# The second rope product of the attention scores: 64 rows or all 128

## The chip, the cores and the metric

The kernel runs on one core of one Trainium2 chip. The metric is the time of one execution on the device in microseconds; several runs are made and their median counts.

## The reference, cut to what matters

The reference is one layer of a decoder: two token mixers side by side (multi-head latent attention and a gated delta rule), merged by gates, then a SwiGLU feed-forward layer, each behind a normalised and modulated input. There is one sequence of 512 tokens, the model width is 2048, and all inputs are f32. The change touches one sum, the attention scores:

```python
MLA_HEADS = 8; QK_NOPE = 128; QK_ROPE = 64; Q_BLOCK = 128
for i in range(T // Q_BLOCK):
    q0, k_end = i * Q_BLOCK, (i + 1) * Q_BLOCK
    s = (jnp.einsum('bqhd,bkhd->bhqk', q_nope[:, q0:k_end], k_nope[:, :k_end])
         + jnp.einsum('bqhr,bkr->bhqk', q_pe[:, q0:k_end], k_pe[:, :k_end]))
    s = s.astype(jnp.float32) * scale
    ...
    p = jax.nn.softmax(jnp.where(mask, s, -jnp.inf), axis=-1).astype(v.dtype)
    outs.append(jnp.einsum('bhqk,bkhd->bqhd', p, v[:, :k_end]))
```

Each head has 128 "nope" features of its own and 64 "rope" features whose key side, `k_pe`, is shared by all heads. The second einsum, over the 64 rope features, is where the change lies.

## The kernel before, in words

All products run on TensorE in the type `float32r`. To keep f32 accuracy a value is split into a high part that `float32r` holds exactly and a low part, the remainder (`hilo`, L235, `halves`, L257). A product of two split operands is then three matmuls: high by high, high by low, low by high (`three`, L273).

The rope features are laid out differently. The 64 features of one head fill only half of the 128 partitions, so the kernel uses the other half for the low part of the queries. For an even head, `qpT[h]` (the tile named `qe`, L1086 to L1092) holds the high part in rows 0 to 63 and the low part, brought there by a DMA, in rows 64 to 127. For an odd head (`qo`) it is the other way round. The keys' side, the tile `kp`, has `kpT[0]`, the high part of `k_pe` in both halves, and `kpT[1]`, its low part in both halves (L1033 to L1042). So one matmul over 128 rows with `kpT[0]` gives the high and the low part of the queries times the high part of the keys. A second matmul gives the high part of the queries times the low part of the keys: before the change it takes only the 64 rows `r` that hold the high part.

Attention is a generator, `attention` (L1142). It runs over 32 items (8 heads by 4 blocks of 128 queries), and one step of it issues the value product of item i-3 (`values`, tile `yT`), the transposes of item i-2 (`transposes`, tile `pT`), the softmax of item i-1 (`softmax`, tiles `sm` and `P`) and the scores of item i (`scores`, tile `sc`). The scores are five matmuls into one PSUM tile: three over the nope features (`qn` by `kn`) and two over the rope features (`qe` or `qo` by `kp`). The moving operand has 256, 256, 384 or 512 columns for the four query blocks of a head.

The generator does not run by itself. Weights stream through units of matmuls (`Unit`, `Driver`, L35 to L127), and after every `GROUP` = 12 matmuls of units the driver advances each open generator by one step:

```python
            for m in u.mms:
                m()
                self.count += u.weight
                if self.count >= GROUP:
                    self.count -= GROUP
                    self.pump()
```

During attention these units are first those of the query and key products (`qk_unit`, tile `qk`), then those of the second gate's logits (tile `gb`), whose four PSUM banks are emptied by ScalarE (`gate_done`, tile `sg`, L1223). Between them stand a few one-column products (`adac`). TensorE, GpSimd and the queue on SyncE keep the order in which the program issues; VectorE and ScalarE are ordered by the tile scheduler. Behind attention come the output products `ya`, `yb` and `wo`, and then the feed-forward layer, most of it as products named `m`. Before it, the gated delta rule uses products on 32x32 and 64x64 parts of the array (tiles `M` and `X`) for its triangular inverse.

Every matmul is recorded at L155, the line of the helper that keeps the order, so the groups of the profile are told apart by their tiles.

Of the kernel before, what the change touches and what calls it, by code (L numbers as in the profile page):

```python
# [171 lines left out]
def block_kernel(ctx: ExitStack, tc: tile.TileContext, a: dict, out, out_t):  # L172
# [17 lines left out]
    def S(s, dt=F32):  # L190
        return slots.tile([P, 512], dt, tag="s", name=nm(s))

    def PS(s):
        return psum.tile([P, 512], F32, tag="ps", name=nm(s))
# [10 lines left out]
    mm = nc.tensor.matmul  # L205

    def tok(j):
        return slice(j * P, (j + 1) * P)
# [26 lines left out]
    def hilo(src, name, scale=None):  # L235
        hi, lo = S(name + "h", F32R), S(name + "l", F32R)
        n = src.shape[1]
        if scale is None:
            nc.scalar.copy(hi[:, 0:n], src)  # L239
            nc.vector.tensor_tensor(lo[:, 0:n], src, hi[:, 0:n].bitcast(F32), ALU.subtract)  # L240
        else:
            nc.scalar.activation(hi[:], src, AF.Copy, scale=scale)
            nc.vector.scalar_tensor_tensor(lo[:], src, scale, hi[:].bitcast(F32), op0=ALU.mult, op1=ALU.subtract)
        return hi, lo
# [750 lines left out]
    kpT = []  # L995
# [49 lines left out]
    qpT = {}  # L1045
# [96 lines left out]
    def attention():  # L1142
        items = [(h, qb) for h in range(8) for qb in range(4)]
        n = len(items)
        box = [dict() for _ in items]
        yps = {}

        def scores(i):
            h, qb = items[i]
            N = max(qb + 1, 2) * P  # L1150
            ps = PS("sc")
            for q, k in ((0, 0), (0, 1), (1, 0)):
                mm(ps[:, 0:N], QN[h][q][:, tok(qb)], KN[h][k][:, 0:N], start=q == k, stop=False)
            r = slice(64, 128) if h % 2 else slice(0, 64)
            mm(ps[:, 0:N], qpT[h][:, tok(qb)], kpT[0][:, 0:N], start=False, stop=False)
            mm(ps[:, 0:N], qpT[h][r, tok(qb)], kpT[1][r, 0:N], start=False, stop=True)
            box[i]["ps"] = ps
            if qb == 3:
                del QN[h], KN[h]

        def softmax(i):
            h, qb = items[i]
            N = (qb + 1) * P
            ps = box[i].pop("ps")
            m, s, r = (sm[:, i, j:j + 1] for j in range(3))
            nc.vector.tensor_tensor(ps[:, tok(qb)], ps[:, tok(qb)], neg, ALU.add)
            nc.vector.tensor_reduce(m, ps[:, 0:N], AX.X, ALU.max)
            nc.vector.tensor_scalar(m, m, -scale, None, op0=ALU.mult)
            p = S("P")
            nc.scalar.activation(p[:, 0:N], ps[:, 0:N], AF.Exp, bias=m, scale=scale, accum_out=s)  # L1170
            nc.vector.reciprocal(r, s)
            nc.vector.tensor_scalar(p[:, 0:N], p[:, 0:N], r, None, op0=ALU.mult)
            box[i]["p"] = p

        def transposes(i):
            h, qb = items[i]
            N = (qb + 1) * P
            p = box[i].pop("p")
            ps = PS("pT")
            for kb in range(qb + 1):  # L1180
                nc.tensor.transpose(ps[:, tok(kb)], p[:, tok(kb)], ident)
            s = S("pT")
            (nc.scalar.copy if i % 2 else nc.vector.tensor_copy)(s[:, 0:N], ps[:, 0:N])
            box[i]["pT"] = s

        def values(i):
            h, qb = items[i]
            s = box[i].pop("pT")
            if qb == 0:
                yps[h] = PS("yT")  # L1190
            for kb in range(qb + 1):
                mm(yps[h][:, tok(qb)], V[h // 4][kb][:, tok(h % 4)], s[:, tok(kb)], start=kb == 0, stop=kb == qb)
            if qb == 3:
                yT[h] = hilo(yps.pop(h)[:], "y")
                if h % 4 == 3:
                    del V[h // 4]

        for i in range(n + 3):
            if i < n:
                while items[i][0] not in QN or items[i][0] not in qpT:  # L1200
                    yield
                if i == 0:
                    yield 2
            if i >= 3:
                values(i - 3)
            if 2 <= i < n + 2:
                transposes(i - 2)
            if 1 <= i < n + 1:
                softmax(i - 1)
            if i < n:  # L1210
                scores(i)
            yield
# [1188 lines left out]
```

## Time and profile before

| | us |
|---|---|
| median of 3 runs | 2759.52 |
| lowest and highest run | 2758.9 and 2764.0 |
| the profiled execution's own time | 2765.03 |
| its span, first to last instruction | 2763.3 |

| engine | busy us | share |
|---|---|---|
| PE (TensorE matmuls) | 2733.2 | 99% |
| PEld (weight loads, beside them) | 2344.3 | 85% |
| DVE (VectorE) | 2016.5 | 73% |
| ACT (ScalarE) | 1171.4 | 42% |
| POOL (GpSimd) | 254.6 | 9% |

How to read it: times are microseconds from the first instruction unless marked ns. A row of the order of time gives start, duration, engine, line, operation, tiles (out<-in), the part of the array that is used (rows*columns), the output's shape and a count; neighbours of one kind are merged. What stands in brackets is the idle time of the engine before the row and who ended it. Matmuls are pipelined: the durations of neighbours overlap and their ends are modelled, so the distance between starts tells what one costs. A group of instructions has busy time, the mean ns of one, and the idle time before it. A tile's view has minimum, median and maximum of the duration in ns. A row of waits has the total, how many, and the longest. A row of windows has the stretch, its length, then the busy time of PE, PEld, DVE, ACT and POOL (with counts), the granted TensorE clock, the DMA share and GB/s.

### The profile page before, as it was taken

To read this page: it belongs to the slowest core of one execution; us is meant where nothing else is said; L and a number is where in the kernel's file an instruction comes from. 1 tells how busy PE (TensorE), PEld (TensorE's weight loads), DVE (VectorE), ACT (ScalarE), POOL (GpSimd) and SP (SyncE) were. 2 spreads that over 40 slices of the span, in tenths; PEclk is the share of its full clock that TensorE was granted. 3 is DMA by queue.
4 is the path that set the end of the run, shared out by engine and by line. 5 is a ranking of instruction groups with operands and counts; after the bars stand their busy time and mean duration, and the time that the engine had idled before them with its cause. 6 is when DMAs were issued, how large, how long until landed. Compare 5 with 4: busy or idle time off the path is not lost.

```text
span 2763.3 us, 39805 instructions
## 1 busy us (share of the span) xinstructions
PE 2733.2 (99%) x14860; PEld 2344.3 (85%) x14860; DVE 2016.5 (73%) x3192; ACT 1171.4 (42%) x1652; POOL 254.6 (9%) x340
## 2 busy tenths in 40 slices
PE   9999999999999999999999999999999999999998
PEld 7888788888888888888999888888888888998997
DVE  8884657676967546784487877778777867878866
ACT  3443432542344333222374444444444445446545
POOL 0000011102000000001000000000000103113113
PEclk9999999999999999999999999999999999999999
DMA  9896556646755648885464655665665668569565
GB/s 358 305 362 200 153 162 180 188 147 181 210 156 161 202 131 289 298 300 200 158 187 135 199 199 198 206 216 198 203 208 191 214 207 193 114 197 204 128 188 166
DMA packets 308924, 558.98 MB, mean 202 GB/s; under 512 B 40085, under 2 KB 109877, under 8 KB 308601
## 3 DMA queue, kind: packets, MB, share of 16 engines
q1 hardware_dynamic: 259848, 461.09, 51.6%
q0 software_dynamic: 29088, 67.42, 9.4%
q10 hardware_dynamic: 19792, 27.92, 2.9%
q8 instruction: 116, 1.90, 0.3%
q14 instruction: 80, 0.65, 0.1%
HBM read 474.52 MB, written 80.76 MB: 201 GB/s over the span
## 4 chain that ended last, share of the span: by engine, by line
PE 93%; DVE 2%; DMA 2%; issue 1%; ACT 1%; POOL 0%; SPq 0%; ACTq 0%; DVEq 0%; POOLq 0%
PE m L155 38%; PE wo L155 6%; PE gb L155 6%; PE v L155 4%; PE gu L155 3%; PE z L155 3%; PE ya L155 3%; PE k L155 3%; PE dn L155 3%; PE q L155 3%; PE yb L155 3%; PE s L155 3%; PE qk L155 2%; PE ckv L155 2%; PE cq L155 2%; PE ga L155 1%
## 5 line engine op out<-in xcount | busy, mean ns | idle before, releaser
L263 ACT CAST hi<-raw 128x1024 fp32r<-128x1024 f32 (+1 forms) x274 | 285.1, 1042 | 663.9 <-DMA raw<-in_w_in_dram 143.7
L264 DVE TENSOR_TENSOR lo<-raw,hi 128x1024 fp32r<-128x1024 f32 (+1 forms) x274 | 337.1, 1232 | 305.9 <-ACT hi L263 289.5
L1727 ACT CAST hi<-raws 128x512 fp32r<-128x512 f32 (+1 forms) x240 | 218.4, 910 | 328.3 <-PE m L155 264.5
L1728 DVE TENSOR_TENSOR lo<-raws,hi 128x512 fp32r<-128x512 f32 (+1 forms) x240 | 247.8, 1045 | 85.2 <-ACT hi L1727 84.7
L155 PE MATMUL m<-xh,hi 128*128 128x256 f32 x896 | 256.4, 286 | 4.2 <-ACT xh L239 2.3
L155 PE MATMUL m<-xl,hi 128*128 128x256 f32 x896 | 256.6, 286 | 3.9 <-DVE xl L240 3.9
L155 PE MATMUL m<-xh,lo 128*128 128x256 f32 x896 | 256.3, 286 | 0.9 <-DVE lo L1903 0.9
L435 DVE CUSTOM_DVE_ANT_0 rawm<-rawm,cbc 128x1024 f32<-128x1024 f32 x192 | 233.0, 1233 | 8.1 <-DMA rawm<-in_w_mod_dram 7.5
L155 PE MATMUL m<-hi,h2h 128*128 128x512 f32 x480 | 190.4, 397 | 0.0
L155 PE MATMUL m<-hi,h2l 128*128 128x512 f32 x480 | 187.2, 390 | 0.0
L155 PE MATMUL m<-lo,h2h 128*128 128x512 f32 x480 | 186.8, 389 | 0.0
L155 PEld LDWEIGHTS m<-xl,hi 128*128 128x128 f32 x896 | 174.8, 195 | 4.8 <-DVE xl L240 4.8
L155 PEld LDWEIGHTS m<-xh,hi 128*128 128x128 f32 x896 | 174.5, 195 | 4.9 <-ACT xh L239 2.7
L155 PEld LDWEIGHTS m<-xh,lo 128*128 128x128 f32 x896 | 174.6, 195 | 1.3 <-DVE lo L1903 1.3
L1727 ACT CAST hi<-sums 128x1024 fp32r<-128x1024 f32 x80 | 84.2, 1053 | 108.8 <-PE m L155 103.9
L1728 DVE TENSOR_TENSOR lo<-sums,hi 128x1024 fp32r<-128x1024 f32 x80 | 97.8, 1223 | 24.1 <-ACT hi L1727 23.6
L155 PE MATMUL wo<-mh,hi 128*128 128x512 f32 (+1 forms) x320 | 111.2, 347 | 0.0
L155 PE MATMUL wo<-ml,hi 128*128 128x512 f32 (+1 forms) x320 | 110.9, 347 | 0.0
L155 PE MATMUL wo<-mh,lo 128*128 128x512 f32 (+1 forms) x320 | 110.9, 347 | 0.0
L1902 ACT CAST hi<-sums 128x1024 fp32r<-128x1024 f32 x64 | 67.1, 1048 | 96.8 <-PE m L155 77.3
L155 PEld LDWEIGHTS m<-hi,h2l 128*128 128x128 f32 x480 | 90.0, 188 | 19.3
L155 PEld LDWEIGHTS m<-lo,h2h 128*128 128x128 f32 x480 | 90.3, 188 | 17.7
(537 smaller groups left out, 7307.8 us busy)
## 6 DMA issues: line engine op xcount, KB each, us to landing
raws<-in_w_gate_up_dram SPq DMA_DIRECT2D x400, 256.0 KB, 3.5
rawm<-in_w_mod_dram SPq DMA_DIRECT2D x192, 512.0 KB, 5.4
raw<-in_w_in_dram SPq DMA_DIRECT2D x144, 512.0 KB, 4.6
raws<-in_w_down_dram SPq DMA_DIRECT2D x128, 256.0 KB, 4.0
raw<-in_w_o_dram SPq DMA_DIRECT2D x40, 512.0 KB, 4.6
s_dram<-raws POOLq DMA_DIRECT2D x80, 256.0 KB, 2.3
raws<-s_dram SPq DMA_DIRECT2D x80, 256.0 KB, 3.2
rawa<-in_w_in_dram SPq DMA_DIRECT2D x32, 512.0 KB, 4.2
```

The source lines that it names most:

```text
L155: return self.tc.keep_in_program_order(f(*args, **kwargs))
L263: nc.scalar.copy(hi[:], raw[:])
L264: (lo_eng or nc.vector).tensor_tensor(lo[:], raw[:], hi[:].bitcast(F32), ALU.subtract)
L435: r = nc.vector.tensor_tensor_reduce(raw, raw, c, 1.0, 0.0, ALU.mult, ALU.add, parts[:, k, half:half + 1])
L1727: nc.scalar.copy(hi[:], src)
L1728: nc.vector.tensor_tensor(lo[:], src, hi[:].bitcast(F32), ALU.subtract)
L1902: nc.scalar.copy(hi[:], src)
```

## The change

In `scores`, the second rope matmul takes all 128 rows of `qpT[h]` and `kpT[1]`, as the first one does with `kpT[0]`. It thereby adds the product of the queries' low part with the keys' low part, a term that was left out before. Nothing else differs.

```diff
-            r = slice(64, 128) if h % 2 else slice(0, 64)
-            mm(ps[:, 0:N], qpT[h][:, tok(qb)], kpT[0][:, 0:N], start=False, stop=False)
-            mm(ps[:, 0:N], qpT[h][r, tok(qb)], kpT[1][r, 0:N], start=False, stop=True)
+            for k in range(2):
+                mm(ps[:, 0:N], qpT[h][:, tok(qb)], kpT[k][:, 0:N], start=False, stop=k == 1)
```

## The prediction

> **What bounds the kernel now.** I read the page first: busy shares, the slices, the chain that ended last.
>
> ```profile
> span 2763.3 us, 39805 instructions
> PE 2733.2 (99%) x14860; PEld 2344.3 (85%) x14860; DVE 2016.5 (73%) x3192; ACT 1171.4 (42%) x1652; POOL 254.6 (9%) x340
> PE 93%; DVE 2%; DMA 2%; issue 1%; ACT 1%; POOL 0%; SPq 0%; ACTq 0%; DVEq 0%; POOLq 0%
> ```
>
> TensorE is busy 99% of the span and makes 93% of the chain. A nanosecond taken from its stream counts unless another engine is late there. So the question is local: what do the 32 score products cost on TensorE, and is anything close behind?
>
> Next the tile view of the scores (sc) gives their shapes and their place, the windows of that stretch who is busy beside them, and the waits of TensorE over the whole span what it ever stops for.
>
> ```profile
> L155 PE MATMUL sc<-knl,qnh x32: 279/310/387, 853.9 to 1006.9; 128*128 128x256 f32 x16, 128*128 128x384 f32 x8, 128*128 128x512 f32 x8
> L155 PE MATMUL sc<-kp,qe x32: 278/380/500, 854.1 to 985.2; 128*128 128x256 f32 x8, 64*128 64x256 f32 x8, 128*128 128x384 f32 x4, 64*128 64x384 f32 x4
> L155 PE MATMUL sc<-kp,qo x32: 278/381/498, 873.0 to 1007.7; 128*128 128x256 f32 x8, 64*128 64x256 f32 x8, 128*128 128x384 f32 x4, 64*128 64x384 f32 x4
> ...
> 853.00:873.00 20.00, 20.00 (x108) 16.36 (x107) 16.26 (x49) 11.56 (x27) 2.08 (x4) 1.00 0.59 174
> 893.00:910.00 17.00, 17.00 (x86) 13.55 (x86) 14.34 (x38) 7.65 (x17) 0.00 (x0) 1.00 0.88 290
> 853.70:1008.20 154.50, 154.16 (x795) 124.36 (x793) 92.42 (x259) 59.71 (x130) 1.82 (x4) 1.00 0.50 162
> ...
> PE m L155 <- DVE xl L240: 3.9, 4, 1.2
> PE gb L155 <- ACT sg L1223: 0.3, 1, 0.3
> ```
>
> There are 32 score products of five matmuls each, 16 with 256 columns, 8 with 384, 8 with 512. The fifth is the one that works on 64 rows (64*128). In their 154.5 us TensorE is busy 154.16 at full clock (1.00), VectorE 92.42, ScalarE 59.71. The only wait of TensorE recorded there is the 0.3 us on sg.
>
> **What the change adds and removes.** Instructions: none either way. Each engine has the same list in the same order in both programs; the only rows that differ are the fifth score matmuls and their weight loads, which become 128*128. No wait, buffer or transfer moves: the added half of qe or qo is what the fourth matmul, just before, reads already, and the added half of kp was written long before.
>
> What a 64-row matmul costs must be read from the distance between starts, since the durations of pipelined matmuls overlap. The order of time around one score product of each width:
>
> ```profile
> 931.21 0.28 PE L155 MATMUL sc<-knh,qnl 128*128 128x256 f32 x1
> 931.33 0.59 PE L155 MATMUL sc<-kp,qe 128*128 128x256 f32 x2
> 931.85 0.50 PE L155 MATMUL gb<-hh,hi 128*128 128x512 f32 x1
> 932.19 0.39 PE L155 MATMUL gb<-hl,hi 128*128 128x512 f32 x1
> 932.42 0.40 PE L155 MATMUL gb<-hh,lo 128*128 128x512 f32 x1
> ...
> 941.79 0.34 PE L155 MATMUL sc<-knh,qnl 128*128 128x384 f32 x1
> 941.97 0.71 PE L155 MATMUL sc<-kp,qe 128*128 128x384 f32 x2
> 942.61 0.50 PE L155 MATMUL gb<-hh,hi 128*128 128x512 f32 x1
> 942.94 0.40 PE L155 MATMUL gb<-hl,hi 128*128 128x512 f32 x1
> ...
> 907.19 0.39 PE L155 MATMUL sc<-knh,qnl 128*128 128x512 f32 x1
> 907.42 0.83 PE L155 MATMUL sc<-kp,qe 128*128 128x512 f32 x2
> 908.18 0.50 PE L155 MATMUL gb<-hh,hi 128*128 128x512 f32 x1
> 908.52 0.40 PE L155 MATMUL gb<-hl,hi 128*128 128x512 f32 x1
> ```
>
> The row "x2" holds the fourth (128 rows) and the fifth matmul (64 rows) together. At 256 columns a full-row step is 931.33 - 931.21 = 0.12, more exactly half of 0.23, since 512 columns take 932.42 - 932.19 = 0.23. The pair takes 931.85 - 931.33 = 0.52 where two full-row steps would take 0.23: 0.29 too much. At 384 columns: 942.61 - 941.97 = 0.64 against 2 x 0.175 (a step is 0.18 by the rows, 0.75 x 0.23 by the columns): 0.29. At 512: 908.18 - 907.42 = 0.76 against 0.46: 0.30. The excess does not grow with the columns, so it is a fixed cost of going in and out of 64 rows, not a slower stream.
>
> Then the first matmul behind it also takes too long: 932.19 - 931.85 = 0.34, 942.94 - 942.61 = 0.33 and 908.52 - 908.18 = 0.34 for 512 columns that cost 0.23. That is another 0.10. Does this second part belong to the 64 rows, or to any change of product? Two other places tell:
>
> ```profile
> 540.93 0.39 PE L155 MATMUL v<-hh,lo 128*128 128x512 f32 x1
> 541.25 2.08 PE L155 MATMUL M<-T,LT 64*64 64x64 f32 x32
> 543.25 0.50 PE L155 MATMUL v<-hh,hi 128*128 128x512 f32 x1
> 543.59 0.39 PE L155 MATMUL v<-hl,hi 128*128 128x512 f32 x1
> ...
> 1040.81 0.39 PE L155 MATMUL gb<-hh,lo 128*128 128x512 f32 x1
> 1041.04 0.39 PE L155 MATMUL ya<-yh,hi 128*128 128x512 f32 x1
> 1041.26 0.39 PE L155 MATMUL ya<-yl,hi 128*128 128x512 f32 x1
> ```
>
> Going from gb to ya, both on 128 rows, costs nothing: 0.23, then 0.22. Going from v into the 64*64 products costs 541.25 - 540.93 = 0.32 in place of 0.23, and the first matmul after them takes 543.59 - 543.25 = 0.34. So both tolls, about 0.09 on entering and 0.11 after leaving, come with the change of the array's shape; the rest, about 0.20, lies on the 64-row matmul itself. With 128 rows all of it should go.
>
> Sum: 16 x (0.29 + 0.11) + 8 x (0.29 + 0.10) + 8 x (0.30 + 0.10) = 6.4 + 3.1 + 3.2 = 12.7 us. Twice the next work is not a 512-column product but adac:
>
> ```profile
> 936.68 1.05 PE L155 MATMUL adac<-ones,acc 128*128 128x1 f32 x8
> ```
>
> There I drop the 0.10, since no row shows it behind that kind: 12.5 us. Bounds of the leaving toll: if it stays in all 30 other items, 9.5; nothing lets it be more than the row shows.
>
> Off this comes what TensorE cannot keep. Two places have cover only just long enough:
>
> ```profile
> 986.87 0.39 PE L155 MATMUL gb<-hh,lo 128*128 128x512 f32 x1
> 987.60 0.50 PE L155 MATMUL gb<-hh,hi 128*128 128x512 f32 x1 [0.34 <-ACT sg L1223]
> ...
> 905.97 0.35 DVE L1172 TENSOR_SCALAR P<-P,sm 128x256 f32<-128x256 f32 x1
> 906.52 0.38 PE L155 MATMUL pT<-kc,P 128*128 128x128 f32 x2
> ```
>
> At 987.60 TensorE waits for ScalarE to empty a bank of the gate product. It already stands still there, so the 0.4 us won in the last score before it only lengthens that wait: minus 0.4. At 906.52 the transposes of P start 906.52 - 906.32 = 0.20 us after VectorE finished P. VectorE is at 16.26 of 20 and 14.34 of 17 us there, 81 and 84%, and it runs in step with TensorE (it begins a softmax when a score is done), so most of its work comes earlier too. Price between 0 (it follows fully) and 4.7 us (all 12 items up to 908 us lose their 0.39). I take 0.4, one item's gain: the cover is thin only at such single rows, and VectorE would still be at about 92% (14.34 over 17 less 3.6 items of 0.4). Behind the stretch nothing consumes the lead: buffers free earlier and loads start earlier by the same amount, and no further TensorE wait of weight exists but those of the m products at the end (3.9 us in all), which follow TensorE's own order.
>
> Net: 12.5 - 0.4 - 0.4 = 11.7 us. The profiled execution took 2765.03 us (span 2763.3 and 1.7 around it), 5.5 over the median of the runs, 2759.52; it would take 2753.3. The part of the program that the change touches is the same in each run, so the median goes to 2759.5 - 11.7 = **2747.8 us**.
>
> **Rivals.**
>
> *VectorE paces the first twelve items.* If the softmax and the splits for the qk units cannot follow, those keep their old pace: 12.5 - 4.7 - 0.4 = 7.4 us, time 2752.1. For it: the 0.20 us of cover, and 81 to 84% busy. Against it: no wait of TensorE on VectorE is recorded there now, and VectorE's own idle time ends mostly when TensorE gives it something.
>
> *Nothing happens.* One matmul with fewer rows costs what a full one costs, and the excess comes from something that stays, such as the reading of kp. Then the time stays at 2759.5. The groups by shape speak against it:
>
> ```profile
> L155 PE MATMUL sc<-kp,qe 64*128 64x256 f32 x8 | 3.0, 380 | 0.0
> L155 PE MATMUL sc<-kp,qe 128*128 128x256 f32 x8 | 2.2, 279 | 0.0
> ```
>
> Both read kp and qe over 256 columns; the 64-row one is 101 ns longer. The Trainium skill, "TensorE: Matmul & The Clock Gate", section "Why this matters for your kernels", has the rule behind this rival: a single matmul with small K takes the same time as one with K=128. By it the sum would be zero; the trace does not bear it out between full-row neighbours.
>
> *Slower: new waits halve the clock.* At its end the kernel shows what short waits can do. There TensorE waits on the m products (the rows above, up to 1.2 us each), and in the window around it the clock falls:
>
> ```profile
> 2338.20:2348.40 10.20, 8.14 (x43) 7.93 (x44) 7.99 (x13) 4.70 (x8) 0.00 (x0) 0.67 0.27 75
> ```
>
> A mean of 0.67 over 10.2 us loses 3.4 us. If TensorE now overruns P in the first twelve items and stands for a microsecond at several of them, each such place could cost 3.4 us. The gain is used up at four of them; slower by more than 5.5 us needs 11.7 + 5.5 = 17.2 us, five or more: 2765 us. Against it: a wait can only grow to what TensorE has won since VectorE was last level, 0.4 us an item, and 0.4 us waits such as that at 987.60 left the clock at 1.00.
>
> **How the numbers follow.** A measurement of this kernel can tell 0.2%, 5.5 us, from no change. The forecast (10 to 13 us won) gets 0.76, VectorE's pace 0.14, nothing 0.07, slower 0.03. The first two are faster by over 0.2% (7.4 us is 0.27%): 0.90; same 0.07; slower 0.03. The range: its low end takes the full 12.5 (2747.0) and 3 us for one half-clock stretch less at the kernel's end; the runs before lie 5.1 us apart (2758.9 to 2764.0), so this is within their play. Its high end takes in the VectorE rival (2752.1) and about 2 us of that play: 2744 to 2754.
>
> **What would show each step.** Right: all 64 kp rows 128*128; the pair at 256 columns takes 0.23 instead of 0.52 and the next first step 0.23 instead of 0.34; the stretch from first to last score shrinks from 154.5 to about 143 us; the sg wait grows from 0.3 to about 0.7. VectorE's pace shows as waits of pT on P in the qk half with the gb half fully shortened. The forecast is wrong if the pair shortens but the 0.34 stays, if new TensorE waits in the stretch sum to over 4 us, or if the stretch shrinks and time behind 1008 us grows.

## The result and the profile after

| | kernel before, us | changed kernel, us |
|---|---|---|
| median of 7 runs each | 2764.42 | 2755.55 |
| lowest and highest run | 2758.9 and 2766.03 | 2751.16 and 2756.55 |
| span of the profiled execution | 2763.3 | 2751.1 |

The ratio of the runs is 0.9968, with a 95% interval from 0.9957 to 0.998: the change makes the kernel faster by about 9 us, between 5.5 and 12. The direction was forecast, and 11.7 us lies within that interval. The time was not: 2755.55 lies over the range of 2744 to 2754. The median of before, 2759.52 from three runs when the prediction was made, is 2764.42 with the four later ones.

The page of the changed kernel, its first lines:

```profile
span 2751.1 us, 39805 instructions
PE 2719.3 (99%) x14860; PEld 2341.4 (85%) x14860; DVE 2016.4 (73%) x3192; ACT 1170.4 (43%) x1652; POOL 255.0 (9%) x340
```

The number of instructions is the same, VectorE and ScalarE are busy as before, and TensorE is busy 13.9 us less (2733.2 before). The tile view of the scores shows the new shape, and the order of time around three score products (the same as were shown of before) the new steps:

```profile
L155 PE MATMUL sc<-kp,qe x32: 278/308/398, 853.9 to 976.2; 128*128 128x256 f32 x16, 128*128 128x384 f32 x8, 128*128 128x512 f32 x8
...
926.57 0.40 PE L155 MATMUL sc<-kp,qe 128*128 128x256 f32 x2
926.80 0.40 PE L155 MATMUL gb<-hh,hi 128*128 128x512 f32 x1
927.04 0.40 PE L155 MATMUL gb<-hl,hi 128*128 128x512 f32 x1
...
936.75 0.51 PE L155 MATMUL sc<-kp,qe 128*128 128x384 f32 x2
937.10 0.39 PE L155 MATMUL gb<-hh,hi 128*128 128x512 f32 x1
937.33 0.40 PE L155 MATMUL gb<-hl,hi 128*128 128x512 f32 x1
...
904.41 0.62 PE L155 MATMUL sc<-kp,qe 128*128 128x512 f32 x2
904.88 0.40 PE L155 MATMUL gb<-hh,hi 128*128 128x512 f32 x1
905.11 0.39 PE L155 MATMUL gb<-hl,hi 128*128 128x512 f32 x1
```

The pair of rope products takes 0.23, 0.35 and 0.47 us, where it took 0.52, 0.64 and 0.76, and the first matmul behind it 0.24, 0.23 and 0.23 instead of 0.33 to 0.34. That is 0.39 or 0.40 us an item at every width, as added up.

The waits of TensorE in this stretch show what was not kept:

```profile
PE gb L155 <- ACT sg L1222: 0.7, 1, 0.7
PE pT L155 <- DVE sm L1167: 0.7, 1, 0.7
PE pT L155 <- DVE P L1171: 0.6, 2, 0.4
```

The wait on sg grew from 0.3 to 0.7, and the transposes of P now wait on VectorE, 1.3 us in all. The sum of the stretch stands between two rows, the first score and the first `ya` (before: 853.70 and 1041.04; from the unrounded starts the distance is 187.33):

```profile
853.45 0.36 PE L155 MATMUL sc<-knh,qnh 128*128 128x256 f32 x1
...
1030.52 0.39 PE L155 MATMUL ya<-yh,hi 128*128 128x512 f32 x1
```

1030.52 - 853.45 = 177.07: the stretch is 10.26 us shorter. From the first score to the last the distance is 144.08 us instead of 154.01.

### The profile page after: what moved, and what is told of

It is laid out like the page before. It is cut to its first block, busy times and chain, and to the rows that moved or that the text cites. A ratio compares the mean times of both kernels' runs of the same rounds, so it can differ in the third digit from the quotient of the medians.

```text
span 2751.1 us, 39805 instructions
## 1 busy us (share of the span) xinstructions
PE 2719.3 (99%) x14860; PEld 2341.4 (85%) x14860; DVE 2016.4 (73%) x3192; ACT 1170.4 (43%) x1652; POOL 255.0 (9%) x340
## 4 chain that ended last, share of the span: by engine, by line
PE 92%; DVE 3%; DMA 2%; issue 1%; ACT 1%; POOL 0%; SPq 0%; DVEq 0%; ACTq 0%; POOLq 0%
PE m L155 38%; PE wo L155 6%; PE gb L155 6%; PE v L155 4%; PE gu L155 3%; PE z L155 3%; PE ya L155 3%; PE k L155 3%; PE dn L155 3%; PE q L155 3%; PE yb L155 3%; PE s L155 3%; PE ga L155 2%; PE ckv L155 2%; PE cq L155 2%
## 5 line engine op out<-in xcount | busy, mean ns | idle before, releaser
L155 PEld LDWEIGHTS m<-hi,h2h 128*128 128x128 f32 x480 | 90.1, 188 | 18.4 <-DVE euvw L1744 0.8
```

The costliest lines, as they stand in the source:

```text
L155: return self.tc.keep_in_program_order(f(*args, **kwargs))
```

## The experiments

Two measures are used. The **stretch** is the distance from the first score to the first `ya` in the trace of one execution; it came out as 187.33 us in all three traces of the unchanged kernel that were taken, so beside it differences of a few tenths can be read. The changed kernel waits more in it, and its three traces lie 0.63 us apart: smaller differences from it, of one trace each, are not read. The **time** of whole runs spreads over 7 us and more, so only ratios of several runs count there.

| kernel | stretch, us | against 187.33 |
|---|---|---|
| before, three traces | 187.33 | 0 |
| changed, three traces | 177.07, 176.49, 176.44 | -10.26 to -10.89 |
| 96 rows | 176.49 | -10.84 |
| 32 rows | 187.08 | -0.25 |
| 64-row matmul twice | 192.17 | +4.84 |
| 128-row matmul twice | 180.32 | -7.01 |
| 64-row matmul first | 187.06 | -0.27 |
| 128 rows from head 3 on | 180.14 | -7.19 |
| changed, one item more of distance | 176.26 | -11.07 |
| changed, P scaled on ScalarE | 176.79 | -10.54 |

**Both kernels again, on two chips.** No edit.

> The kernel before, unchanged, to see how its runs lie. Theory clock: the runs differ by how long TensorE stood at half clock, so a span grows by 0.0005 x 2763 = 1.4 us for each 0.001 by which the mean clock is lower if half of the work is lost in it, up to 2.8 us if all of it is; runs at 0.997 near 2759, runs at 0.994 or 0.995 near 2766, and the median of many runs near 2764, not 2759.5. Rival draw: the clock is the same in short and long runs, the spread is of another source, and the median of many goes back to 2759.5.

> The changed kernel, unchanged. Theory toll: 10 us less than the kernel before in the same rounds, ratio 0.9963 with an interval from 0.995 to 0.998; runs from 2750 to 2757. Rival nothing: ratio within 0.2% of 1.

The kernel before had a median of 2765.45 us (11 runs, 2763.11 to 2771.26) beside 2764.68 (21 runs, from 2759.77) of the same program in the same rounds. The changed kernel had 2753.79 (5 runs, 2749.19 to 2757.74), ratio 0.9963, interval 0.995 to 0.9975. Then the same on another chip:

> The kernel before once more, on whichever chip comes. If the low runs of 2758.9 and 2759.5 were the luck of three draws, the median is again 2764 to 2766 and at most one run in ten lies below 2760. If they belong to the chip or the day, another median can come out, down to 2759.5.

> The changed kernel once more beside it: 10 to 11 us under the kernel before of the same rounds, ratio 0.996, whatever its level.

Before: 2764.1 (10 runs, 2761.27 to 2769.97) beside 2763.91 (15 runs, from 2761.72). Changed: 2753.6 (6 runs, 2750.19 to 2757.22), ratio 0.9968, interval 0.9955 to 0.998. Of these 57 runs of the kernel before, on two chips, one lies under 2760 us. The two low runs among the three that the prediction started from, 2758.9 and 2759.52, were a rare draw, or came from a chip that was not met again; that can't be told apart. The mean clock of the 57 runs goes with their time as the theory said (2769.2 us on average at 0.994, 2766.3 at 0.995, 2763.0 at 0.997), but the runs at 0.997 lie near 2763, not 2759 as it had said.

Where the spread of the runs arises can be seen in two traces of the same program. Windows of the feed-forward layer, first of `base` and then of `base_b`:

```profile
1490.80:2330.00 839.20, 839.20 (x3838) 697.35 (x3837) 651.46 (x762) 383.79 (x466) 87.06 (x140) 1.00 0.63 203
2330.00:2763.00 433.00, 409.60 (x3088) 395.19 (x3086) 334.62 (x530) 214.84 (x325) 78.27 (x94) 0.97 0.62 164
```

```profile
1490.80:2330.00 839.20, 839.12 (x3832) 696.23 (x3831) 650.53 (x761) 383.50 (x466) 86.83 (x140) 1.00 0.63 203
2330.00:2768.00 438.00, 414.12 (x3094) 399.40 (x3092) 335.19 (x532) 215.44 (x326) 78.17 (x94) 0.96 0.62 163
```

Up to 2330 us the two run alike, at full clock. From there to the end the first takes 431.3 us and the second 436.6 (the windows reach 1.7 and 1.4 us past the end), at mean clocks of 0.97 and 0.96: a difference of 5 us that has nothing to do with the scores. A mean clock lower by 0.01 over 435 us loses 4.4 us, so within the rounding of these two rows the clock accounts for it; up to the last matmul the trace records 13.7 us at half clock in the one and 23.9 us in the other, 10.2 us more. In `base`, from 2341.8 to 2345.2 us, products of 256 columns start every 213 ns at half clock, and right behind it every 120 ns, so 44% of such time is lost: 4.5 us of the 5, by this estimate. That is 2.4 us for each 0.001 of mean clock, nearer to the upper of the two prices that the theory named. Over all 14 traces the time at half clock goes from 6.8 to 23.9 us and the way from the first `m` behind the stretch to the start of the last matmul from 1255.7 to 1263.0 us, both lowest in one trace (`full_b`) and both highest in another (`base_b`). Five traces with 17.1 us at half clock still lie between 1259.6 and 1262.9. There the idle time of TensorE differs, from 9.3 us in the shortest to 11.9 in the longest; without it all five take 1250.3 to 1251.0 us. What decides on the number of half-clock stretches is open.

**Is it the row count or the array's shape?** In the fifth matmul the rows are set to 96 or 32:

```diff
-            r = slice(64, 128) if h % 2 else slice(0, 64)
+            r = slice(0, 96)                                        # 96 rows
+            r = slice(64, 96) if h % 2 else slice(0, 32)            # 32 rows
```

> The kernel before with the fifth score matmul over rows 0 to 95 in place of 64 (the sum leaves out the last 32 rows, or for odd heads takes half of the high part). Theory toll: what costs is the change of the array's shape, and 96 rows need the full one: recorded as 96*128, but with the steps of the changed kernel (pair at 256 columns 0.23, next first step 0.23), lead 10 us. Rival row: fewer than 128 rows cost, whatever the shape: the pair stays at 0.52.

> The kernel before with the fifth score matmul over 32 rows in place of 64 (half of the low keys' term is left out). Theory toll: a fixed price for leaving the full shape, the same for 32 as for 64 rows: pair 0.52 at 256 columns, next step 0.34, time as the kernel before within 1 us. Rival row: the excess goes with the rows left out, half as much again: pair about 0.67.

The order of time with 96 rows, then with 32. A merged row has the shape of its first matmul, so the tile view of the 96-row kernel stands ahead; it lists the fifth matmul as 96*128:

```profile
L155 PE MATMUL sc<-kp,qe x32: 278/310/398, 853.5 to 975.3; 128*128 128x256 f32 x8, 96*128 96x256 f32 x8, 128*128 128x384 f32 x4, 96*128 96x384 f32 x4
...
925.66 0.41 PE L155 MATMUL sc<-kp,qe 128*128 128x256 f32 x2
925.90 0.40 PE L155 MATMUL gb<-hh,hi 128*128 128x512 f32 x1
926.13 0.40 PE L155 MATMUL gb<-hl,hi 128*128 128x512 f32 x1
```

```profile
931.33 0.59 PE L155 MATMUL sc<-kp,qe 128*128 128x256 f32 x2
931.85 0.50 PE L155 MATMUL gb<-hh,hi 128*128 128x512 f32 x1
932.18 0.40 PE L155 MATMUL gb<-hl,hi 128*128 128x512 f32 x1
```

With 96 rows the pair takes 0.24 and the next step 0.23, as with 128; with 32 rows 0.52 and 0.33, as with 64. The stretch is 176.49 and 187.08. So a row count of less than 128 costs nothing by itself, and the price does not grow with the rows left out: it is the same at 64 and 32 rows and absent at 96. This is read as a price for changing the array's shape, where 96*128 counts as the full shape; that it does is inferred from its steps. The single runs, 2756.28 and 2765.22 us beside 2765.18 of the kernel before, agree.

**Does each 64-row matmul pay, or each change of shape?** The fifth matmul is issued twice, in the kernel before and in the changed one:

```diff
-            mm(ps[:, 0:N], qpT[h][r, tok(qb)], kpT[1][r, 0:N], start=False, stop=True)
+            mm(ps[:, 0:N], qpT[h][r, tok(qb)], kpT[1][r, 0:N], start=False, stop=False)
+            mm(ps[:, 0:N], qpT[h][r, tok(qb)], kpT[1][r, 0:N], start=False, stop=True)
```

> The kernel before with its fifth score matmul (64 rows) issued twice in a row; the output has that term twice. Theory toll: the cost is one way into and out of the 64-row shape, so the second one costs only its columns, 16 x 0.115 + 8 x 0.175 + 8 x 0.229 = 5.1 us in all over the kernel before. Rival row: each 64-row matmul is slow by about 0.2 us by itself, so 5.1 + 32 x 0.2 = 11.5 us in all.

> The changed kernel with its fifth score matmul (128 rows) issued twice; the output has that term twice. Both theories: 5.1 us over the changed kernel, steps of 0.115, 0.175 and 0.229 us for the added ones. It is the yardstick for the doubled 64-row one.

The order of time of the first, in two views, the second of which begins at the 64-row matmuls:

```profile
934.17 0.70 PE L155 MATMUL sc<-kp,qe 128*128 128x256 f32 x3
934.81 0.50 PE L155 MATMUL gb<-hh,hi 128*128 128x512 f32 x1
```

```profile
934.38 0.50 PE L155 MATMUL sc<-kp,qe 64*128 64x256 f32 x2
934.81 0.50 PE L155 MATMUL gb<-hh,hi 128*128 128x512 f32 x1
935.15 0.40 PE L155 MATMUL gb<-hl,hi 128*128 128x512 f32 x1
```

Three products take 0.64 where two took 0.52: the second 64-row matmul adds 0.12, the price of its columns. The stretch grows by 4.84 us (5.1 expected of the toll, 11.5 of the rival; the wait of 0.3 us on sg is gone from that trace). The doubled 128-row one adds only 3.25 to 3.88 over the changed kernel, not 5.1: the waits of pT on VectorE, worth 1.4 to 2.0 us in the changed kernel (see below), are gone from that trace, since TensorE is slower there and overruns nothing. The single runs took 2767.24 and 2759.41 us.

This run also mends the prediction's division of the toll. In nanoseconds, starts to starts at 256 columns, the fourth matmul takes 209, the first 64-row one 223, the second 206, and the first 512-column one behind 335 to 338. Against 117 and 229 the excess is 92, 106, 89 and 106 to 109. So one change of shape costs about 0.09 us ahead of it and 0.11 in the first matmul after it, 0.20 in all, and an item has two changes, in and out. The single 64-row matmul carries the second part of the one and the first part of the other; it has no price of its own.

The rows of the weight loads (PEld) show what happens at such a change. First the kernel before, with the first two `gb` matmuls behind a 64-row one, then the changed kernel with the first of them:

```profile
931.85 0.19 PEld L155 LDWEIGHTS gb<-hh,hi 128*128 128x128 f32 x1
931.85 0.50 PE L155 MATMUL gb<-hh,hi 128*128 128x512 f32 x1
931.96 0.19 PEld L155 LDWEIGHTS gb<-hl,hi 128*128 128x128 f32 x1
932.19 0.39 PE L155 MATMUL gb<-hl,hi 128*128 128x512 f32 x1
...
926.69 0.19 PEld L155 LDWEIGHTS gb<-hh,hi 128*128 128x128 f32 x1
926.80 0.40 PE L155 MATMUL gb<-hh,hi 128*128 128x512 f32 x1
```

Without a change of shape the weights of a matmul are loaded beside the matmul ahead of it: 0.23 us before its own start for `hl,hi`, 0.11 us for `hh,hi` in the changed kernel. Behind the 64-row matmul the load begins only with its own matmul. In the stretch of the kernel before this is so at all 64 changes (the load is 1 or 2 ns ahead), while the median of the other matmuls is 223 ns. With 96 rows, and at the second of two 64-row matmuls, the load runs ahead again (median 144 ns). A load at a change takes 183 to 186 ns, so the 0.20 us of a change are close to one weight load that nothing covers; that they are nothing else is not shown.

**Does the place matter?** The 64-row matmul goes first, right behind the transposes of P:

```diff
+            mm(ps[:, 0:N], qpT[h][r, tok(qb)], kpT[1][r, 0:N], start=True, stop=False)
+            mm(ps[:, 0:N], qpT[h][:, tok(qb)], kpT[0][:, 0:N], start=False, stop=False)
             for q, k in ((0, 0), (0, 1), (1, 0)):
-                mm(ps[:, 0:N], QN[h][q][:, tok(qb)], KN[h][k][:, 0:N], start=q == k, stop=False)
+                mm(ps[:, 0:N], QN[h][q][:, tok(qb)], KN[h][k][:, 0:N], start=False, stop=q == 1)
...
```

> The kernel before with the order of the five score matmuls turned: the 64-row one first, right behind the transposes, then the 128-row rope product, then the three nope products. In the kernel before the first nope product already takes 0.20 in place of 0.12 us behind the transposes. Theory toll, not shared: the 64-row shape costs its 0.39 us wherever it stands, the stretch from the first score to the first ya stays at 187.3 us within 0.5. Theory toll, shared: the entry falls together with that pause behind the transposes and 0.08 to 0.09 us an item are saved, 184.5 us. Rival place: the excess belonged to the end of the accumulation, and with a full-row product last it goes: 177 us.

```profile
930.89 0.70 PE L155 MATMUL sc<-kp,qe 64*128 64x256 f32 x2
931.43 0.28 PE L155 MATMUL sc<-knh,qnh 128*128 128x256 f32 x1
931.55 0.28 PE L155 MATMUL sc<-knl,qnh 128*128 128x256 f32 x1
931.66 0.28 PE L155 MATMUL sc<-knh,qnl 128*128 128x256 f32 x1
931.78 0.40 PE L155 MATMUL gb<-hh,hi 128*128 128x512 f32 x1
932.02 0.39 PE L155 MATMUL gb<-hl,hi 128*128 128x512 f32 x1
```

The pair takes 0.54 at its new place, and the way to gb is now free (0.24). The stretch, which now begins with a 64-row matmul, is 187.06 us, 0.27 less, within the 0.5 that was allowed for and far from 184.5 and 177 (one run, 2761.67 us): the toll moves with the 64-row matmul and is not shared with the pause behind the transposes.

**Where the gain comes from, and what VectorE takes back.** 128 rows only from head 3 on:

```diff
-            r = slice(64, 128) if h % 2 else slice(0, 64)
+            r = slice(0, 128) if h >= 3 else slice(64, 128) if h % 2 else slice(0, 64)
```

> 128 rows only for heads 3 to 7 (the last 20 of 32 items, those beside gb); the first 12 items keep 64 rows. Theory toll: each of the 20 items wins 0.39 us, no item loses it to VectorE, the sg wait takes 0.4: a lead of about 7.3 us behind the stretch and 7.3 us less time than the kernel before. Rival pace: if the first 12 items win nothing that lasts in the changed kernel either, this one equals the changed kernel, 10 us.

The stretch is 180.14 us, 7.19 shorter, and the only wait in it is sg:

```profile
PE gb L155 <- ACT sg L1223: 0.7, 1, 0.7
```

The time is 2758.95 (11 runs), ratio 0.9979, interval 0.997 to 0.9988, 5.8 us less by the ratio, between 3.3 and 8.3; the toll said 7.3, and the rival's 10 lies outside. So the last 20 items bring 7.2 us and the first 12, in the changed kernel, 10.3 to 10.9 less 7.2, or 3.1 to 3.7 us, where the prediction had counted 4.7. What is missing there goes with the wait of pT on VectorE, which this kernel does not have.

Two attempts to remove that wait follow. In the first, the transposes and the value product come one item later:

```diff
-        for i in range(n + 3):
+        for i in range(n + 4):
...
-            if i >= 3:
-                values(i - 3)
-            if 2 <= i < n + 2:
-                transposes(i - 2)
+            if i >= 4:
+                values(i - 4)
+            if 3 <= i < n + 3:
+                transposes(i - 3)
```

> The changed kernel with the transposes of P and the value products one item later, so that VectorE has one more step (some 4.4 us) for a softmax. Theory cover: the waits of pT on VectorE (1.3 us, and about 0.2 us before a yT) go, the lead of TensorE behind the stretch grows from 10.1 to between 11.3 and 12.0 us, and the time is 1 to 2 us under the changed kernel. Rival rate: VectorE is late because it has too much work in the qk half, the waits come back at another row, and the lead stays at 10.1 us.

The waits of pT are gone, and two others stand in their place:

```profile
PE sc L155 <- DVE knl L240: 1.3, 1, 1.3
PE gb L155 <- DVE yl L240: 0.6, 1, 0.6
```

The stretch is 176.26 us, 0.2 below the better traces of the changed kernel; the time, 2755.54 (5 runs), ratio 0.9969 with an interval from 0.9956 to 0.9981, is not lower. The "cover" theory said 11.3 to 12.0 us of lead and missed with 11.07; the waits came back at other rows of VectorE, as the rival had said, whose 10.1 missed too. In the second attempt P is scaled on ScalarE:

```diff
-            nc.vector.tensor_scalar(p[:, 0:N], p[:, 0:N], r, None, op0=ALU.mult)
+            nc.scalar.activation(p[:, 0:N], p[:, 0:N], AF.Copy, scale=r)
```

> The changed kernel with the last step of the softmax, the scaling of P by the reciprocal sum, on ScalarE in place of VectorE, which frees about 12 us of VectorE in the stretch. Theory cover: the waits of pT on VectorE (0.6 to 1.3 us) go and the stretch from first score to first ya falls from 176.5 or 177.1 to about 175.8 us; no other wait takes their place. Rival rate: another wait on VectorE (a split for the next head) shows up instead and the stretch stays at 176.5 or more; ScalarE being late would show as waits of pT on ScalarE.

```profile
PE pT L155 <- ACT P L1171: 0.6, 1, 0.6
```

Now pT waits on ScalarE, and the stretch is 176.79 (one run, 2755.04 us). That is what the rival had named, 176.5 or more and waits of pT on ScalarE; the 175.8 of the "cover" theory did not come. The wait changed its owner and its size stayed. As far as one trace of each can tell, neither a lighter VectorE nor one item more of distance does away with it alone. What the whole chain of softmax and splits would need to keep pace in the qk half stays open; no version tried can be told from the changed kernel in time.

## Why the prediction was right or wrong

**The fixed cost of the 64-row shape: right.** The excess of 0.29 to 0.30 in the pair and 0.10 in the next matmul went in full at every width. That it belongs to the change of shape, which the prediction took from the 64*64 products, is shown by four runs: 96 rows are free, 32 cost what 64 cost, a second 64-row matmul costs only its columns, and another place changes next to nothing. Taken row by row, the changed kernel gains 12.6 to 12.7 us in its three traces before sg and the transposes take back their part; the sum had 12.5. The Trainium skill, "TensorEngine Tiling (Array Packing)", section "Key Properties", says that changing the tiling mode drains the TensorEngine; these runs agree, and put 0.20 us on one change between neighbours that otherwise stream without a gap. The remark that 0.20 lay on the 64-row matmul itself was wrong as a cause: it is the latter half of the way in and the first half of the way out. The sum is not touched by it.

**The rule that few rows cost what many cost.** It was the ground of the rival "nothing happens". The 96-row run agrees with it (0.24 against 0.23 for the pair); between full-row neighbours it fails as soon as the shape changes, with 64 and 32 rows alike.

**What TensorE cannot keep: the places right, the second term too small.** Both named places are the ones where time was lost: sg went from 0.3 to 0.7, the 0.4 that was taken off, and pT waits on VectorE at the qk half. The second was put at 0.4; the waits shown above are 1.3 us, and 0.6 in the two later traces of the changed kernel. Taken from start to start against the kernel before, the transposes lose more, 2.0 us and twice 1.4, at three items between 884 and 913 us. A third place was missed. The prediction let both items that are followed by adac keep their 0.30, and one of them does not:

```profile
931.00 0.40 PE L155 MATMUL sc<-kp,qe 128*128 128x256 f32 x2
931.48 1.05 PE L155 MATMUL adac<-ones,acc 128*128 128x1 f32 x8
...
931.48 0.41 PEld L155 LDWEIGHTS adac<-ones,acc 128*128 128x128 f32 x3 [0.29 <-ACT pT L1182]
```

At 931.48 in the changed kernel the pair before adac still takes 0.48 (0.52 before). The kernel with one item more of distance has 0.24 there:

```profile
930.49 0.40 PE L155 MATMUL sc<-kp,qe 128*128 128x256 f32 x2
930.73 0.50 PE L155 MATMUL adac<-ones,acc 128*128 128x1 f32 x4
```

The row of the weight load names what held adac: its load stood idle for 0.29 us until ScalarE had copied pT. So of 12.5 us, 10.3 to 10.9 remain rather than 11.7. The VectorE rival had the right mechanism with the wrong reach: VectorE takes back 1.4 to 2.0 us, not the 4.7 of all twelve items.

**Where the gain goes behind the stretch: right.** From the first `ya` to the first `m` the three traces of the changed kernel and two of the three of the kernel before take 449.3 us (the third 450.1). Nothing consumes the lead.

**The level: wrong, and this is the step that failed.** The prediction said that the median goes to 2759.5 - 11.7. It knew that the profiled execution lay 5.5 us higher, and took the median of three runs as the level all the same. 57 further runs have medians from 2763.9 to 2765.45. From the profiled execution's own time the same sum gives 2765.03 - 11.7 = 2753.3; the changed kernel's medians are 2755.55, 2753.79 and 2753.6. Of the miss of 7.8 us (2755.55 - 2747.8), 4.9 is the shift of the level (2764.42 - 2759.52) and 2.9 the smaller gain by medians (8.87 instead of 11.7), of which 0.8 to 1.4 is seen in the stretch; the rest lies within the spread of runs. The smaller gain alone would have stayed in the range (2759.52 - 8.87 = 2750.65). The range was made from the same three runs, so it allowed for 2 us of play at its upper end where the runs have 7.

**The slower rival** did not come: the waits on VectorE, up to 0.7 us, left the clock at full, as the window of the changed kernel's stretch shows.

```profile
853.45:1030.50 177.05, 174.94 (x951) 151.06 (x950) 107.30 (x281) 72.08 (x147) 1.82 (x4) 1.00 0.55 181
```

## What to carry to other kernels

In a stream of matmuls that is itself the bottleneck, one matmul on 64 or 32 rows between full-row neighbours is not cheaper but costs two changes of the array's shape, here 0.4 us together, more than the matmul itself at 512 columns; feed it full rows, or 96, or put the small ones next to each other. Read such costs from the distance between starts, and look at the matmul after the odd one as well. And make the level of a prediction from as many runs as there are, the profiled one included: three runs of a kernel that spreads over 7 us do not give it.

## What the runs showed of the hardware

One change of the array's shape cost about 0.20 us at full clock, in two parts: 0.09 ahead of the first matmul in the new shape and 0.11 in that matmul, alike for 32 and 64 rows and in both directions; at the 64*64 products the 0.09 of the way in and the 0.11 of the way out can be read. At such a change the weight load did not run ahead of its matmul. A matmul on 96 rows is recorded as 96*128 and costs none of it. Not expected was how exactly the chip repeats where TensorE hardly waits (0.3 us in all): the 187.33 us of the stretch came out the same to 0.01 us in three traces, while the last 430 us of the kernel, where TensorE waits for microseconds and the clock falls, differ by 5 us between two runs of one program.
